# Squares for the query and key norms of band attention: written to an SBUF tile instead of the block's PSUM

## The chip, the core and the metric

The kernel runs on one core of a Trainium2 chip. The metric is the device time of one execution in microseconds; the lower the better. The kernel before takes 2714.26 us (median of 3 runs, 2714.21 to 2715.04).

## What is computed

A trunk of two layers over 256 tokens of width 2048, all in float32. Each layer is a modulated RMS norm, a token mixer with a gated residual, a second modulated norm and a squared-ReLU MLP with a gated residual. The mixer of the first layer runs two groups of heads side by side behind one input projection: eight gated-DeltaNet heads, and eight heads of chunked band attention. The change touches the start of the attention alone, where queries and keys are normed per head:

```python
def chunk_band_attention(q, k, v, q_norm_w, k_norm_w, rel_bias):
    ...
    qh = rms_norm(heads(q), q_norm_w).astype(f32) * (ATT_DH ** -0.5)
    kh = rms_norm(heads(k), k_norm_w).astype(f32)
    ...

def rms_norm(x, w):
    xf = x.astype(jnp.float32)
    y = xf * lax.rsqrt(jnp.mean(xf * xf, axis=-1, keepdims=True) + NORM_EPS)
    return (y * w.astype(jnp.float32)).astype(x.dtype)
```

The mean of squares runs over the 128 channels of one head. Of the squares themselves nothing but these sums is used.

## The kernel before

Weights stream from HBM in pieces of 1 MB through four SBUF buffers (`raw`, SP's queue). Each half of a piece is split into a rounded part `wh` (ScalarE, L317) and a remainder `wl` (VectorE, L321), and TensorE multiplies in three passes (wh by u, wl by u, wh by the remainder of u), all through the helper at L308. Between the weights, VectorE works off the rows of the modulation matrix (`mraw`, L439), each a multiply with a sum over 128x2048.

A projection of 512 columns for 256 tokens is a block. It lands in one PSUM tile `pg` of two banks, one for each 128 tokens; there are two such tiles (pool `psg`), so a third block must wait until the first one's tile is read out. A generator per block (a task) is then stepped along between the matmuls of the following blocks, so that its ScalarE and VectorE work lies beside them. Program order sets priorities; a scheduler then places every instruction on its engine's queue, and the engines run their queues in order.

`att_qk` (L1232) is that task for a block of queries or keys of four heads. It runs four times: for AQ and AK, whose blocks carry a partial sum from earlier (`part`, added by VectorE at L1242), and for AQ+1 and AK+1, whose blocks are copied by ScalarE (L1240). For each half t of 128 tokens it brings the block into an SBUF tile `aq` and takes the squares of four heads (L1244), with the sum of each into a column of the small tile `ass`. The squares go back into the half of the block that has just been read. When both halves are done, VectorE makes the reciprocal root of the eight sums (L1247, then L271 to L276 in three Newton rounds), scales `aq` (L1250), TensorE transposes it (L314, `pm<-ident,aq`) and ScalarE takes the result to SBUF (L1257).

At the same time the DeltaNet heads run in `gdn_tile`: their squares for norms are L1042, the gates `gu` L1046, and their blockwise inversion takes a fresh tile `gY` per level, cleared by GpSimd (L1107). All of these, `aq` among them, come from one pool of 18 SBUF tiles of 2 KB per partition (`s2`): a nineteenth has to wait until one of the 18 has been read for the last time.

Of the kernel before, what the change touches and what calls it, by code (L numbers as in the profile page):

```python
# [13 lines left out]
AF = mybir.ActivationFunctionType  # L14
# [4 lines left out]
P = 128  # L19
# [93 lines left out]
class Trunk:  # L113
# [1118 lines left out]
    def att_qk(self, ps, nw, part=None):  # L1232

        nc = self.nc
        a, v = [], self.small(8, "ass")
        for t in range(2):
            x = self.s2(tag="aq")
            flat = x.rearrange("p h d -> p (h d)")
            if part is None:
                nc.scalar.copy(flat, ps[t])  # L1240
            else:
                nc.vector.tensor_tensor(flat, ps[t], part[:, t], op=ALU.add)  # L1242
            for h in range(4):
                nc.scalar.activation(ps[t][:, h * P : h * P + P], x[:, h], AF.Square, accum_out=v[:, t * 4 + h : t * 4 + h + 1])  # L1244
            a.append(x)
            yield
        nc.vector.tensor_scalar(v, v, 1.0 / P, EPS, op0=ALU.mult, op1=ALU.add)  # L1247
        r = self.rsqrt(v, 8, "a")
        for t in range(2):
            nc.vector.tensor_tensor(a[t], a[t], self.bc(r[:, t * 4 : t * 4 + 4]), op=ALU.mult)  # L1250
        yield
        res = self.unit()
        for t in range(2):
            pt = self.pm()
            for h in range(4):
                self.tr(pt[:, h], a[t][:, h])
            nc.scalar.activation(res[:, :, t * P : t * P + P], pt, AF.Copy, scale=nw)  # L1257
            if t == 0:
                yield
        return res  # L1260
# [551 lines left out]
```

## Time and profile before

| | before |
|---|---|
| median of 3 runs | 2714.26 us |
| the profiled execution | 2719.37 us |
| its span, first to last instruction | 2717.6 us |
| TensorE busy | 2665.0 us (98%) |
| VectorE busy | 2147.6 us (79%) |
| ScalarE busy | 1351.2 us (50%) |
| the 32 squares of `att_qk` | first at 240.0, last at 409.2 us |

Times within the profile count from the start of its span. Busy time is time in which an engine has an instruction under way; the idle time before an instruction is put down to what released it. TensorE's clock is told as a share of full speed (1.00 is 2.4 GHz, 0.50 is 1.2 GHz).

### The profile page before, as it was taken

The page shows a single profiled execution, that of the slowest core. Times are in us where ns is not written, and L with a number is a line of the kernel's source. Part 1 is how long each engine was busy: PE and PEld are TensorE (multiplying, and loading weights), DVE is VectorE, ACT ScalarE, POOL GpSimd, SP SyncE. Part 2 cuts the span into 40 slices and gives each one's busy share as a digit, 9 for nine tenths or more (in the row PEclk, how much of TensorE's full clock was granted, in tenths as well). Part 3 has the DMA queues.
Part 4 walks back from the last instruction along what each step waited for, and adds up shares of the span by engine and source line. Part 5 has one row for each costly group of instructions (what it writes and reads, how often), then busy time and mean ns, then how long its engine had stood idle before and what let it go on. Part 6 is the DMA issues. An engine that isn't in the chain of part 4 may idle for free.

```text
span 2717.6 us, 39677 instructions
## 1 busy us (share of the span) xinstructions
PE 2665.0 (98%) x15664; PEld 2350.4 (86%) x15664; DVE 2147.6 (79%) x3081; ACT 1351.2 (50%) x1976; POOL 24.5 (1%) x98
## 2 busy tenths in 40 slices
PE   5999999999999999999999999999999999999999
PEld 5887989888888888888888888888888888888888
DVE  7998998987888888889889876897777855555554
ACT  3444454546445354454556544665555354454452
POOL 1000000000000000000000000000000000000000
PEclk9999999999999999999999999999999999999999
DMA  9986487867899898988456665554558855555554
GB/s 341 353 325 235 172 301 272 294 241 282 322 339 328 328 336 330 333 331 307 165 185 217 217 234 200 203 185 172 196 177 293 324 201 188 188 191 193 186 192 134
DMA packets 100459, 680.06 MB, mean 250 GB/s; under 512 B 11185, under 2 KB 14513, under 8 KB 19377
## 3 DMA queue, kind: packets, MB, share of 16 engines
q1 hardware_dynamic: 95376, 669.07, 68.5%
q10 hardware_dynamic: 4896, 8.46, 1.0%
q8 instruction: 123, 2.02, 0.3%
q14 instruction: 64, 0.52, 0.1%
HBM read 675.33 MB, written 2.16 MB: 249 GB/s over the span
## 4 chain that ended last, share of the span: by engine, by line
PE 90%; DVE 6%; DMA 1%; ACT 1%; issue 1%; SPq 0%; ACTq 0%; DVEq 0%
PE pw L308 70%; PE pg L308 13%; PE pm L311 4%; PE pm L308 3%; DVE mraw L439 2%; DVE wl L321 1%; PE pm L314 1%; DMA mraw<-in_mod_dram 1%; DVE u L1592 0%; ACT wh L317 0%; DVE hf L862 0%; ACT pm L1042 0%; DMA raw<-in_w_ab_dram 0%; DMA x<-in_x_dram 0%; DVE u L865 0%
## 5 line engine op out<-in xcount | busy, mean ns | idle before, releaser
L317 ACT CAST wh<-raw 128x1024 fp32r<-128x1024 f32 x870 | 907.1, 1051 | 1031.6 <-PE pw L308 732.9
L321 DVE TENSOR_TENSOR wl<-raw,wh 128x1024 fp32r<-128x1024 f32 x870 | 1048.7, 1220 | 463.8 <-ACT wh L317 349.6
L308 PE MATMUL pw<-u,wh 128*128 128x512 f32 x5584 | 1321.6, 391 | 2.6 <-DVE pad L973 1.9
L308 PEld LDWEIGHTS pw<-u,wh 128*128 128x128 f32 x5584 | 1032.2, 188 | 208.2 <-issue 3.3
L308 PEld LDWEIGHTS pw<-u,wl 128*128 128x128 f32 x5584 | 702.3, 191 | 21.3 <-issue 2.1
L308 PE MATMUL pw<-u,wl 128*128 128x256 f32 x5584 | 714.5, 283 | 0.3 <-DVE wl L321 0.3
L439 DVE SCALAR_TENSOR_TENSOR mraw<-mraw,crow 128x2048 f32<-128x2048 f32 x192 | 438.0, 2283 | 17.8 <-DMA mraw<-in_mod_dram 17.5
L308 PE MATMUL pg<-wh,u 128*128 128x512 f32 x864 | 281.6, 397 | 0.0
L308 PEld LDWEIGHTS pg<-wh,u 128*128 128x128 f32 x864 | 161.9, 188 | 32.1 <-issue 0.5
L925 DVE SCALAR_TENSOR_TENSOR x<-pw,mod,x 128x256 f32<-128x256 f32 x352 | 161.1, 478 | 22.6 <-PE pw L308 20.3
L308 PE MATMUL pg<-wl,u 128*128 128x512 f32 x432 | 169.9, 393 | 0.7 <-DVE wl L321 0.5
L308 PE MATMUL pg<-u,wh 128*128 128x256 f32 x672 | 124.6, 285 | 0.0
L308 PEld LDWEIGHTS pg<-u,wh 128*128 128x128 f32 x672 | 105.7, 192 | 0.3
L308 PEld LDWEIGHTS pg<-wl,u 128*128 128x128 f32 x432 | 81.4, 188 | 17.6 <-DVE wl L321 2.1
L308 PE MATMUL pg<-u,wl 128*128 128x256 f32 x336 | 95.3, 284 | 0.0
L308 PE MATMUL pm<-u,wh 128*128 128x256 f32 (+1 forms) x304 | 64.6, 310 | 19.2 <-ACT wh L317 19.2
L308 PEld LDWEIGHTS pm<-u,wh 128*128 128x128 f32 x304 | 49.1, 198 | 20.3 <-ACT wh L317 20.0
L308 PEld LDWEIGHTS pg<-u,wl 128*128 128x128 f32 x336 | 64.4, 192 | 0.1
L984 DVE SCALAR_TENSOR_TENSOR u<-pad,cst,u 128x256 f32<-128x256 f32 x144 | 60.6, 477 | 3.3 <-ACT u L978 3.2
L864 ACT ACTIVATE u<-hf,mod 128x256 fp32r<-128x256 f32 x64 | 29.3, 502 | 53.0 <-DVE hf L862 53.0
L1504 ACT ACTIVATE rl<-rs 128x512 f32<-128x512 f32 x64 | 40.4, 632 | 18.9 <-DVE rs L1499 14.4
L308 PE MATMUL pm<-u,wl 128*128 128x256 f32 x176 | 46.1, 290 | 3.1 <-DVE wl L321 3.1
(299 smaller groups left out, 1580.5 us busy)
## 6 DMA issues: line engine op xcount, KB each, us to landing
raw<-in_w_dram SPq DMA_DIRECT2D x256, 1024.0 KB, 5.0
mraw<-in_mod_dram SPq DMA_DIRECT2D x192, 1024.0 KB, 6.0
raw<-in_w_ab_dram SPq DMA_DIRECT2D x56, 1024.0 KB, 5.7
raw<-in_w_ssd_dram SPq DMA_DIRECT2D x48, 1024.0 KB, 4.9
raw<-in_w_sz_dram SPq DMA_DIRECT2D x32, 1024.0 KB, 4.9
raw<-in_wo_ssd_dram SPq DMA_DIRECT2D x32, 1024.0 KB, 4.8
raw<-in_wo_ab_dram SPq DMA_DIRECT2D x16, 1024.0 KB, 5.2
sE<-sd_rowd ACTq DMA_DIRECT2D x32, 256.0 KB, 4.9
```

The source lines that it names most:

```text
L308: self.nc.tensor.matmul(o, a, b, start=start, stop=stop, skip_group_check=True)
L311: self.nc.tensor.matmul(o, lhsT, rhs, start=True, stop=True, skip_group_check=True)
L314: self.nc.tensor.transpose(o, a, self.ident[:k, :k])
L317: a = self.nc.scalar.copy(hi, src)
L321: b = self.nc.vector.tensor_tensor(lo, src, hi.bitcast(F32), op=ALU.subtract)
L439: x = nc.vector.scalar_tensor_tensor(raw, raw, 1.0, self.crow, op0=ALU.mult, op1=ALU.mult, accum_out=t[:, f : f + 1])
L864: nc.scalar.activation(hi, h[:, f], AF.Identity, bias=shift[:, col])
L925: nc.vector.scalar_tensor_tensor(x[:, 2 * b + f], ps[:, f, n], g[:, 2 * cb + f : 2 * cb + f + 1], x[:, 2 * b + f], op0=ALU.mult, op1=ALU.add)
L984: nc.vector.scalar_tensor_tensor(h, pad[:, f, 1 + q : 257 + q], w[:, q, j : j + 1], h, op0=ALU.mult, op1=ALU.add)
L1504: nc.scalar.activation(rl, lo, AF.Relu)
```

## The change

The squares of `att_qk` no longer go back into the block's PSUM tile. They go to an SBUF tile `asq` of the pool of 18, one for each of the four calls, used by both halves in turn. What is squared, the sums, and the number of instructions are the same; each call asks the pool for three tiles instead of two.

```diff
         nc = self.nc
         a, v = [], self.small(8, "ass")
+        sq = self.s2(tag="asq")
         for t in range(2):
             x = self.s2(tag="aq")
...
             for h in range(4):
-                nc.scalar.activation(ps[t][:, h * P : h * P + P], x[:, h], AF.Square, accum_out=v[:, t * 4 + h : t * 4 + h + 1])
+                nc.scalar.activation(sq[:, h], x[:, h], AF.Square, accum_out=v[:, t * 4 + h : t * 4 + h + 1])
             a.append(x)
             yield
```

## Rows read from the trace of the kernel before

**Rows 1.** The page: busy time of an engine, share of the span, instructions.
```profile
PE 2665.0 (98%) x15664; PEld 2350.4 (86%) x15664; DVE 2147.6 (79%) x3081; ACT 1351.2 (50%) x1976; POOL 24.5 (1%) x98
```
**Rows 2.** Windows of the mixer: stretch, its length; busy by engine; clock, DMA share, GB/s.
```profile
240.00:260.00 20.00, 19.42 (x101) 14.31 (x99) 14.09 (x59) 17.59 (x83) 0.53 (x1) 1.00 0.54 201
...
340.00:380.00 40.00, 39.21 (x201) 32.04 (x200) 38.14 (x92) 25.64 (x87) 2.62 (x5) 1.00 0.81 290
...
420.00:440.00 20.00, 17.98 (x143) 17.64 (x142) 14.16 (x28) 6.19 (x9) 0.31 (x1) 0.91 0.79 270
```
**Rows 3.** TensorE's longest waits from 240 to 520 us: total, times, longest.
```profile
PE pm L314 <- DVE aq L1250: 2.8, 2, 2.0
PE pm L314 <- DVE go L1197: 0.5, 1, 0.5
PE pm L311 <- DVE gd_g L1007: 0.4, 1, 0.4
```
**Rows 4.** ScalarE by line and form: busy us, mean ns; idle before.
```profile
L830 ACT ACTIVATE sq<-x 128x512 f32<-128x512 f32 x24 | 14.7, 628 | 17.1 <-DVE x L925 16.8 <-DMA x<-in_x_dram 0.4
...
L1244 ACT ACTIVATE pg<-aq 128x128 f32<-128x128 f32 x32 | 9.0, 281 | 2.2 <-DVE aq L1242 1.8
...
L818 ACT ACTIVATE sq<-x 128x256 f32<-128x256 f32 x16 | 6.4, 415 | 7.1 <-DVE x L925 6.9
```
**Rows 5.** ScalarE's timeline at 240 and 359 us: start, length, instruction, idle before.
```profile
240.04 0.28 ACT L1244 ACTIVATE pg<-aq 128x128 f32<-128x128 f32 x1 [1.80 <-DVE aq L1242]
...
240.48 0.28 ACT L1244 ACTIVATE pg<-aq 128x128 f32<-128x128 f32 x1
...
359.29 0.28 ACT L1244 ACTIVATE pg<-aq 128x128 f32<-128x128 f32 x1
...
359.58 0.27 ACT L1042 ACTIVATE pm<-pm 128x128 f32<-128x128 f32 x1
...
361.02 0.27 ACT L1244 ACTIVATE pg<-aq 128x128 f32<-128x128 f32 x1
```
**Rows 6.** VectorE's timeline around the block AK.
```profile
253.12 0.69 DVE L1242 TENSOR_TENSOR aq<-pg,u 128x512 f32<-128x512 f32 x1 [3.18 <-ACT pg L1244]
254.53 0.17 DVE L1047 TENSOR_SCALAR gss<-gss 128x8 f32<-128x8 f32 x1 [0.72 <-ACT pm L1042]
```
**Rows 7.** Timelines of VectorE, ScalarE and TensorE around the block AQ+1.
```profile
361.45 0.17 DVE L1247 TENSOR_SCALAR ass<-ass 128x8 f32<-128x8 f32 x1 [1.59 <-ACT pg L1244]
...
363.76 1.29 DVE L1250 TENSOR_TENSOR aq<-aq,ay 128x512 f32<-128x512 f32 x2
...
363.60 1.57 ACT L1046 ACTIVATE gu<-Umask,gd_g 128x128 f32<-128x128 f32 x5
...
364.60 0.63 PE L314 MATMUL pm<-ident,aq 128*128 128x128 f32 x4 [0.79 <-DVE aq L1250]
```
**Rows 8.** Timelines of VectorE and TensorE around AK+1's norm.
```profile
411.82 0.16 DVE L1247 TENSOR_SCALAR ass<-ass 128x8 f32<-128x8 f32 x1
...
423.27 2.29 DVE L439 SCALAR_TENSOR_TENSOR mraw<-mraw,crow 128x2048 f32<-128x2048 f32 x1 [2.24 <-DMA mraw<-in_mod_dram]
...
427.94 1.09 PE L314 MATMUL pm<-ident,aq 128*128 128x128 f32 x4 [2.02 <-DVE aq L1250]
```
**Rows 9.** Window behind that wait.
```profile
427.00:432.00 5.00, 4.06 (x23) 4.09 (x24) 3.72 (x6) 1.65 (x3) 0.00 (x0) 0.66 0.78 298
```
**Rows 10.** Timelines of ScalarE, GpSimd and TensorE: AK+1's copies and squares, cleared tiles.
```profile
395.68 0.58 ACT L1240 COPY aq<-pg 128x512 f32<-128x512 f32 x1 [2.95 <-PE pm L311]
...
409.23 0.28 ACT L1244 ACTIVATE pg<-aq 128x128 f32<-128x128 f32 x1
...
400.69 0.52 POOL L1107 MEMSET gY<- 128x512 f32 x1 [5.35 <-PE pm L311]
...
412.85 0.52 POOL L1107 MEMSET gY<- 128x512 f32 x1 [4.67 <-PE pm L311]
...
415.55 0.28 PE L308 MATMUL pg<-u,wh 128*128 128x256 f32 x1
```

## The prediction

> **What bounds the kernel now.** I read the page first, then windows over the stretch in which the changed line runs, then the waits of TensorE in it, and last the timelines around each of the four calls. The page shows TensorE busy for 2665.0 of 2717.6 us, with VectorE at 79% and ScalarE at 50% [rows 1]. So an edit to ScalarE's work moves the end only where TensorE stands still, or runs at its lower clock, because of it. The windows show how little of that there is while the squares run: TensorE stands still for 0.6 us from 240 to 260, 0.8 us from 340 to 380 and 2.0 us from 420 to 440, where the clock is also below full [rows 2]. The list of waits gives the same by cause: 2.8 us in two waits for the scaled `aq`, which is what `att_qk` makes, 0.5 us for the DeltaNet output, and 0.4 us for its gates [rows 3]. That is the whole stock from which the change can draw: 3.7 us of waits, and what the clock costs behind the longest of them.
>
> **The change part by part.** It adds and removes no instruction but the tile; it moves the output of 32 squares, drops what their output held up, and asks the pool of 18 for one tile more in each call.
>
> *The square itself.* Now, from SBUF to PSUM, it takes 281 ns for 128 columns [rows 4]. From SBUF to SBUF the trace has the same function at 415 ns for 256 and 628 ns for 512 columns, so 0.83 ns a column, and 415 - 107 = 308 ns for 128 [rows 4]. That is 27 ns more, 0.9 us for 32. The Trainium skill says the same of direction (ScalarE: Activation LUTs, section "ACT is a hardware spline evaluator": a ScalarE result reaches PSUM sooner than SBUF) and gives no size; by that rule alone the change could only lose.
>
> *The pace of squares.* Two squares of one half that follow each other directly start 0.44 us apart (240.04, 240.48), while a square and the DeltaNet square behind it, which writes another tile, start 0.29 us apart (359.29, 359.58) [rows 5]. I read the difference as each square waiting for the end of the one before it, since both write into one PSUM tile. Counted in ScalarE's timeline, twelve of the 32 follow a sister directly. If quarters of an SBUF tile are kept apart, as I expect, they gain 12 x 0.15 = 1.8 us, against the 0.9 us above. Both lie on ScalarE, which idles half of the time, and count for nothing by themselves.
>
> *The add that waits.* In AK, VectorE stood for 3.18 us until the last square of the first half, and only then added the second half at 253.12 [rows 6]. The add reads the other bank of the tile that the squares write. With the squares gone from the tile it can run some 3 us earlier. I count it at nothing: TensorE has other matmuls here (its one wait before 260 is the 0.4 us for the gates, upstream of the add), and VectorE's next instruction waits for the DeltaNet squares on ScalarE anyway, 0.72 us at 254.53 [rows 3, 6]. The Trainium skill tells (PSUM — Partial Sum Buffer, section "PSUM bank collisions raise a hardware error") that PSUM needs guarding by bank, and the two halves are two banks. By that rule the add had no need to wait for the squares, and the wait would be for something else and stay. The row, which names the squares, speaks for the tile as a whole; the time is the same by both, but it gives the case below in which nothing changes a little more weight.
>
> *The wait at 364.* For AQ+1, TensorE stands 0.79 us until VectorE has scaled `aq` [rows 7]. The chain behind it is: last square, then VectorE released at 361.45 after 1.59 us of waiting for it, the Newton rounds, the scaling at 363.76. Before it, the four squares of the second half alternated with DeltaNet squares, from 359.29 to 361.02, 0.58 us each [rows 5]. Freed from each other they may stand together, at about 0.31 us each: the last would start at 360.2, 0.8 us sooner. At best this ends the 0.79 us. At worst the order stays, and the gain is nothing. What comes next then is the matmul on `gu`, whose last gate ScalarE finishes at 365.2, with TensorE's 0.63 us of transposes before it [rows 7]; the DeltaNet squares and gates that the four pass would end as much later as these end sooner. I take 0.5 us, between the ends, nearer the upper one since the VectorE row names the square as the last to come.
>
> *The wait at 426.* For AK+1, TensorE stands 2.02 us, again for `aq` [rows 8]. Behind it the granted clock is 0.66 over five microseconds, a mean of its levels of 2.4 and 1.2 GHz, so 5 x 0.34 = 1.7 us of work more is lost [rows 9]. But here the last square starts at 409.23, and VectorE takes up the sums 2.3 us after its end, at 411.82, then gets stuck for 2.24 us behind a modulation row whose transfer has not landed, at 423.27 [rows 8, 10]. Squares that end some tenths earlier change nothing in that. I take 0, with 3.7 us as the upper bound.
>
> *The nineteenth tile.* AK+1's first copy, at 395.68, waited 2.95 us for a matmul that has nothing to do with the block it reads: it waited for a tile of the pool, and so do the clearings of `gY`, at 400.69 to 412.85, for 5.35 and 4.67 us [rows 10]. The pool is full here, and a third tile for the call must come out of one of these places. If the call gives way, its squares slip from one release to the next, at most from 409.5 to about 413. The next block, GZ, which takes the PSUM tile, starts at 415.55 [rows 10], and needs after the change only that the copies are through. VectorE's 411.82 becomes some 413.5 at worst, still ahead of the transfer at 423.27. If `gY` gives way, it is a clearing made many microseconds ahead of its use. I take 0; the price if that cover is gone is 1 us.
>
> *The order of everything behind.* The scheduler places the later instructions anew when 32 instructions have other waits. The trace can't show that. Its bounds are the stalls of this stretch: all of them gone (3.7 + 1.7 = 5.4 us gained), or one such as that at 426 more.
>
> The sum is -0.5 us. The profiled execution would go from 2719.37 to 2718.9; it is 5.1 us above the median of the runs, so on the median's scale 2714.26 - 0.5 = 2713.8.
>
> **The rivals.** *Slower: VectorE's queue falls behind a transfer.* If the new order puts one more modulation row ahead of the Newton rounds or of a weight remainder in the stretch 410 to 430, VectorE waits for its landing as at 423.27 (2.24 us) and works it off (2.29 us), TensorE stands for these 4.5 us, and the low clock costs 1.7 us more [rows 8, 9]: 2714.3 + 6.2 = 2720.5. It decides where TensorE has no more finished weights: it ran out of them once in before. For it speaks that this stall exists; against it that the squares' group comes earlier, if at all.
>
> *Faster: the stalls of the stretch go.* With the add, the squares and the release of the block's tile all sooner, VectorE could be ahead by its 3.18 us when the transfer comes late, and both waits for `aq`, the smaller ones and the clock's loss go: 2714.3 - 5.4 = 2708.9. Against it speaks that from 340 to 380 VectorE is at 95% and has no room to carry a lead over 170 us [rows 2].
>
> *The pool.* The third tile holds the call and the inversion up beyond their cover: 2715.3, as priced above.
>
> *Nothing changes.* The squares still wait for each other in the new tile, the add waits for something else, and the order stays: 2714.3. For it speaks that the PSUM tile seems to be guarded as a whole, and the SBUF tile may be too; against it the row of the add, which names the squares [rows 6].
>
> **How the numbers follow.** The forecast, 2713.8 and two or so microseconds around it, has 0.50; nothing changes 0.10; the pool 0.07; slower 0.21; faster 0.12. The range reaches to both outer cases, 2707 to 2721, and leaves out what lies beyond them. A measurement of this kernel can tell about 0.2%, 5.4 us, from no change. Faster by more takes the faster case in full, 0.12; the slower case lies beyond it, 0.21; the rest is 0.67.
>
> **What would show it.** In the profile after, the squares should take about 308 ns each and follow each other 0.3 us apart; the add of AK should no longer wait for them; TensorE's waits for `aq` should be 2 us rather than 2.8, all of it at AK+1. If squares in a row still start 0.44 us apart, my reading of their waits is wrong. If TensorE's waits between 240 and 520 us differ by more than 2 us from 3.7, the order has moved, and the forecast holds only by luck. If the difference lies after 520 us, I missed where the change reaches.

## The result, and the profile after

The changed kernel takes 2722.04 us (median of 11 runs) against 2715.12 us of the kernel before beside it: ratio 1.0024, 95% interval 1.0015 to 1.0034. It is 6.9 us slower, where 0.5 us less was forecast. The execution shown ahead of the prediction was a long one (2719.37 us, with a stretch at the lower clock); the kernel before was profiled once more as e1 (2714.30 us, none such in the mixer), and "before" below means that profile. The profiled execution of after took 2720.30 us; the spans of the two profiles are 2712.6 and 2718.6 us, 6.0 us apart.

First the edited line itself. The fence shows the squares of after as one group (count; duration in ns, least, median and most; first and last start), then three of them in a row, then AK's add:

```profile
L1245 ACT ACTIVATE asq<-aq x32: 292/294/312, 239.7 to 416.0; 128x128 f32<-128x128 f32 x32
...
240.30 0.29 ACT L1245 ACTIVATE asq<-aq 128x128 f32<-128x128 f32 x1
...
240.59 0.29 ACT L1245 ACTIVATE asq<-aq 128x128 f32<-128x128 f32 x1
...
240.88 0.29 ACT L1245 ACTIVATE asq<-aq 128x128 f32<-128x128 f32 x1
...
253.25 0.17 DVE L1047 TENSOR_SCALAR gss<-gss 128x8 f32<-128x8 f32 x1 [4.07 <-ACT pm L1042]
...
254.76 0.68 DVE L1243 TENSOR_TENSOR aq<-pg,u 128x512 f32<-128x512 f32 x1
```

A square takes 294 ns instead of 281, and squares in a row start 0.29 us apart instead of 0.44 [rows 4, 5]. The add no longer waits for them [rows 6]: it now stands behind VectorE's wait for the DeltaNet squares, 4.07 us long, and so it doesn't start sooner (254.76 against 253.12 us). Each local change is small. The loss is elsewhere. Windows of the four stretches from 360 us on (length; busy time and instructions of TensorE, its weight loads, VectorE, ScalarE and GpSimd; TensorE's clock, DMA share, GB/s), before and then after:

```profile
360.00:380.00 20.00, 19.22 (x102) 15.48 (x101) 18.45 (x59) 11.37 (x37) 2.11 (x4) 1.00 0.75 278
380.00:400.00 20.00, 20.00 (x128) 17.62 (x127) 19.39 (x34) 8.13 (x17) 1.57 (x3) 1.00 0.81 301
400.00:420.00 20.00, 20.00 (x163) 19.06 (x162) 19.69 (x34) 9.49 (x19) 2.10 (x4) 1.00 0.91 332
420.00:440.00 20.00, 19.43 (x168) 19.05 (x168) 17.16 (x32) 8.39 (x18) 0.31 (x1) 1.00 0.79 289
```

```profile
360.00:380.00 20.00, 18.85 (x100) 15.14 (x99) 19.20 (x49) 13.18 (x38) 2.62 (x5) 1.00 0.88 327
380.00:400.00 20.00, 19.46 (x102) 15.91 (x100) 19.86 (x40) 3.18 (x4) 1.05 (x2) 1.00 0.81 311
400.00:420.00 20.00, 16.96 (x141) 15.82 (x140) 19.72 (x29) 11.03 (x28) 2.25 (x5) 1.00 0.92 323
420.00:440.00 20.00, 20.00 (x174) 19.62 (x173) 15.52 (x37) 7.38 (x11) 0.68 (x2) 1.00 0.65 233
```

Between 380 and 420 TensorE of before never stands still and issues 291 matmuls; of after it is busy for 36.42 of 40 us and issues 243. The clock is full in both. The first matmul of the output projection shows that the loss lies ahead of it, in before and in after:

```profile
488.32 1.33 PE L308 MATMUL pw<-u,wh 128*128 128x512 f32 x5
```

```profile
495.19 2.00 PE L308 MATMUL pw<-u,wh 128*128 128x512 f32 x8
```

It starts 6.9 us later. From there to the end of the span after takes 2223.4 us and before 2224.2 us, so nothing is added behind it. TensorE's longest waits between 240 and 520 us (us in total, times, longest), in after:

```profile
PE pm L314 <- DVE gX L1114: 2.2, 2, 1.3
PE pm L314 <- ACT gu L1046: 1.1, 1, 1.1
PE pm L314 <- DVE aq L1251: 0.8, 1, 0.8
PE pg L308 <- ACT aq L1241: 0.7, 1, 0.7
```

Before had none of the first [rows 3]: `gX` is the working tile of the DeltaNet inversion (L1107 to L1119), where each step needs the one before. So the question became why the inversion of the second DeltaNet group (heads 4 to 7) is now in the way. The group has two tiles of 128 tokens, and each makes a `gV` (L1069). Right behind the group's second `gV` VectorE makes the inversion's inputs (L1078 to L1082), so that `gV`, called the second `gV` from here on, tells when the inversion can start. VectorE's timeline, before, with the Newton rounds of AQ+1 and of the group's first tile, and then the second `gV`:

```profile
361.88 0.16 DVE L1047 TENSOR_SCALAR gss<-gss 128x8 f32<-128x8 f32 x1
...
362.31 0.16 DVE L274 TENSOR_TENSOR gt<-gy 128x8 f32<-128x8 f32 x1
362.42 0.17 DVE L276 SCALAR_TENSOR_TENSOR ay<-at,ay 128x8 f32<-128x8 f32 x1
362.51 0.16 DVE L275 TENSOR_TENSOR gt<-gt,gn 128x8 f32<-128x8 f32 x1
362.62 0.17 DVE L274 TENSOR_TENSOR at<-ay 128x8 f32<-128x8 f32 x1
...
381.79 0.68 DVE L1069 TENSOR_TENSOR gV<-pm,gnk 128x512 f32<-128x512 f32 x1
```

After:

```profile
364.55 0.16 DVE L274 TENSOR_TENSOR gt<-gy 128x8 f32<-128x8 f32 x1
364.62 2.29 DVE L439 SCALAR_TENSOR_TENSOR mraw<-mraw,crow 128x2048 f32<-128x2048 f32 x1
...
366.83 0.17 DVE L275 TENSOR_TENSOR gt<-gt,gn 128x8 f32<-128x8 f32 x1
366.91 0.69 DVE L1063 TENSOR_TENSOR gE<-gE,Umask 128x512 f32<-128x512 f32 x1
367.51 0.16 DVE L276 SCALAR_TENSOR_TENSOR gy<-gt,gy 128x8 f32<-128x8 f32 x1
367.59 2.29 DVE L439 SCALAR_TENSOR_TENSOR mraw<-mraw,crow 128x2048 f32<-128x2048 f32 x1
...
389.03 0.68 DVE L1069 TENSOR_TENSOR gV<-pm,gnk 128x512 f32<-128x512 f32 x1
```

The Newton rounds are chains of small steps, 0.2 us each. Before, the attention's chain (`ay`, `at`) and the DeltaNet's (`gy`, `gt`) stand between one another, a step every 0.1 us. After, the attention's chain runs alone, and its scaling begins at 363.12; the DeltaNet's comes behind it, and between its steps stand modulation rows of 2.29 us. The group's first `gV` comes 8.9 us later for it (378.13 against 369.27). Counted from the start of the trace, 53 modulation rows and 82 weight remainders stand ahead of the second `gV` in before, 55 and 84 in after. Two of each are 2 x 2.29 + 2 x 1.22 = 7.0 us, and `gV` is late by 389.03 - 381.79 = 7.2 us.

### The profile page after: what moved, and what is told of

It is laid out like the page before. It is cut to its first block, busy times and chain, and to the rows that moved or that the text cites. A ratio compares the mean times of both kernels' runs of the same rounds, so it can differ in the third digit from the quotient of the medians.

```text
span 2718.6 us, 39708 instructions
## 1 busy us (share of the span) xinstructions
PE 2663.3 (98%) x15664; PEld 2347.2 (86%) x15664; DVE 2150.4 (79%) x3081; ACT 1349.9 (50%) x1976; POOL 24.3 (1%) x98
## 3 DMA queue, kind: packets, MB, share of 16 engines
q8 instruction: 123, 2.02, 0.3%
## 4 chain that ended last, share of the span: by engine, by line
PE 90%; DVE 7%; ACT 1%; issue 1%; DMA 1%; SPq 0%; DVEq 0%; ACTq 0%
PE pw L308 70%; PE pg L308 13%; PE pm L311 3%; PE pm L308 3%; DVE mraw L439 2%; DVE wl L321 2%; PE pm L314 1%; DMA mraw<-in_mod_dram 1%; DVE u L1593 0%; ACT wh L317 0%; DVE hf L862 0%; DMA x<-in_x_dram 0%; DVE u L865 0%; DMA sE<-sd_rowd 0%; ACT pm L1042 0%
```

## The experiments

Every median is of 5 to 11 executions, beside the kernel before on the same chip (medians 2714.66 to 2715.53 us). The table gives the median, its ratio to that before with the 95% interval, and from the profile: when the second `gV` starts, how many rows and remainders stand ahead of it, how long TensorE waits for `gX`, `gXt` and `gY` between 380 and 440 us (a sum of rounded rows), and when the output projection begins.

| kernel | us | ratio | gV | rows, rem. | waits | output |
|---|---|---|---|---|---|---|
| e1 before | 2715.12 | 1.0000 (0.9991-1.0009) | 381.8 | 53, 82 | 0 | 488.3 |
| after | 2722.04 | 1.0024 (1.0015-1.0034) | 389.0 | 55, 84 | 2.2 | 495.2 |
| e2 own tile | 2721.14 | 1.0019 (1.0010-1.0027) | 389.6 | 55, 84 | 2.2 | 494.9 |
| e3 last call alone | 2716.01 | 1.0000 (0.9991-1.0009) | 381.8 | 53, 82 | 0 | 487.6 |
| e4 tile held | 2723.58 | 1.0032 (1.0020-1.0045) | 387.4 | 54, 84 | 3.5 | 496.6 |
| e5 one slot | 2718.43 | 1.0006 (0.9997-1.0015) | 382.5 | 53, 82 | 0 | 490.8 |
| e6 AQ+1 alone | 2723.26 | 1.0025 (1.0015-1.0035) | 389.5 | 55, 84 | 3.4 | 495.8 |
| e7 AQ and AK alone | 2716.38 | 1.0004 (0.9995-1.0013) | 382.9 | 53, 82 | 0 | 488.7 |
| e8 before, Newton late | 2723.50 | 1.0029 (1.0018-1.0041) | 389.5 | 55, 84 | 3.4 | 497.1 |
| e9 DeltaNet squares first | 2723.79 | 1.0031 (1.0021-1.0042) | 391.0 | 55, 84 | 2.2 | 498.8 |
| e10 after, rows held | 2732.31 | 1.0070 (1.0057-1.0083) | 370.6 | 47, 79 | 0 | 492.2 |
| e11 before, rows held | 2734.59 | 1.0072 (1.0059-1.0085) | 373.2 | 48, 80 | 2.4 | 494.2 |
| e12 before, Newton first | 2717.32 | 1.0011 (1.0002-1.0020) | 379.8 | 52, 82 | 0 | 491.1 |
| e13 after, pool of 20 | 2720.64 | 1.0023 (1.0015-1.0032) | 389.0 | 55, 84 | 2.5 | 495.2 |
| e14 before, pool of 20 | 2715.61 | 1.0004 (0.9995-1.0012) | 381.9 | 53, 82 | 0 | 489.6 |
| e15 all but AQ+1 | 2715.19 | 1.0002 (0.9993-1.0011) | 382.3 | 53, 82 | 0 | 488.4 |
| e16 before, smaller dose | 2721.59 | 1.0026 (1.0017-1.0035) | 387.2 | 54, 84 | 3.5 | 496.5 |

The theory at the start was ORDER: VectorE's work ahead of the second DeltaNet group is what costs. Its first rival was POOL, the third tile that each call holds.

**e1, the kernel before again.**

> The kernel before once more, with a second profile of it. Both theories: 2714 to 2716 us, ratio 1.000. What it is for: the profiled execution of before took 2719.4 us, 4 us over its own median, with a stretch at the lower clock at 428 and another near 1378 us. If such stretches come and go from execution to execution, this profile shows fewer or other ones, and the stalls of the mixer alone are compared.

It gave the profile that the comparisons use.

**e2, squares in an SBUF tile outside the pool of 18.**

```diff
-        sq = self.s2(tag="asq")
+        sq = self.s_p.tile([P, 4, P], F32, tag="asq", name=self.nm("asq"), bufs=1)
```

> The change, but the squares go to an SBUF tile of their own beside the pool of 18 (2 KB more), so no call asks the pool for a third tile. Theory POOL (the third tile, asked of a full pool, holds up the copies of AK+1 and with them the next block): back to 2714 to 2717 us, the second copy of AK+1 near 407 us and no wait of TensorE for it. Theory ORDER (squares that no longer wait for each other make the scheduler place modulation rows ahead of the DeltaNet's Newton rounds, the second gV comes at 389 instead of 382 us): stays at 2720 to 2724 us, with gV near 389.

The pool has all its tiles back, and the loss stays.

**e3, the change in AK+1 alone.** AK+1 is where the pool is full.

```diff
-put("k1", self.att_qk(ps, self.knw))
+put("k1", self.att_qk(ps, self.knw, None, True))   # own tile for this call
```

> The change in the last of the four calls (AK+1) alone; the other three write into the block's PSUM as before. POOL: nearly the whole loss stays, 2719 to 2722 us, since only there the pool is full; squares of AK+1 start near 407 and its second copy near 414 us. ORDER: the shift of VectorE's queue lies before that call (from 365 us), so it goes: 2714 to 2717 us, second gV near 382 us.

Nothing is lost. With e2 the third tile is out as the main cause.

**e4, the tile held, three of four squares still in PSUM.**

```diff
-activation(ps[t][:, h * P : h * P + P], x[:, h], AF.Square, ...)
+activation(sq[:, h] if h == 3 else ps[t][:, h * P : h * P + P], x[:, h], AF.Square, ...)
```

> Each call takes the third tile of the pool, but three of its four squares per half still go into the block's PSUM and only the fourth into the tile: the tile is asked for and held as in the change, while squares in a row and the second add wait as before. POOL: 2719 to 2724 us. ORDER: 2714 to 2717 us.

A miss for ORDER as I had put it, which expected the old order from a kernel that leaves most squares in PSUM. But its `gV` is late too, with 54 rows and 84 remainders ahead: one square moved is enough to shift the order, so this kernel doesn't separate the theories.

**e5, the change with the squares made to wait for one another.**

```diff
-activation(sq[:, h], x[:, h], AF.Square, ...)
+activation(sq[:, 0], x[:, h], AF.Square, ...)
```

> The change in all four calls, in the pool's tile, but all four squares of a half write the same quarter of asq, so that each has to wait for the one before, as in the kernel before. IN A ROW (the loss comes because the squares of AQ+1 no longer wait for one another: ScalarE's queue then holds four of them in a row ahead of the DeltaNet squares of line 1042, the DeltaNet tiles' Newton rounds start behind AQ+1's instead of between them, and two more modulation rows and four more weight remainders go in): the squares of line 1245 alternate with those of line 1042 again, second gV of the second DeltaNet group at 381 to 383 us, 2714 to 2717 us. TILE (the place matters: SBUF as destination, a tile of the pool of 18 held, the PSUM no longer guarding the add): 2719 to 2724 us, as after.

The order of before is back. The median, 2718.43 us, lies between the two ranges; it is 2.9 us above before, with an interval of the ratio that includes 1. In the profiled execution TensorE waits 2.00 us for AK+1's scaled `aq`, behind a modulation row whose transfer landed 2.21 us late; that is the stall of [rows 8], which comes and goes with the execution.

**e6 and e7, the change in AQ+1 alone, and in AQ and AK alone.**

```diff
-put("q1", self.att_qk(ps, self.qnw))
+put("q1", self.att_qk(ps, self.qnw, None, True))   # e6
-self.att_qk(ps, self.knw if c0 == AK else self.qnw, part)
+self.att_qk(ps, self.knw if c0 == AK else self.qnw, part, True)   # e7
```

> Squares in an SBUF tile in AQ+1 alone; AQ, AK and AK+1 as before. IN A ROW (AQ+1's squares beside the DeltaNet squares): second gV at 388 to 390 us, 2719 to 2724 us. FIRST TWO (the changed calls AQ and AK, over 100 us sooner, shift what follows): second gV near 382, 2714 to 2717 us.

> Squares in an SBUF tile in AQ and AK alone; AQ+1 and AK+1 as before. IN A ROW: second gV at 381 to 383 us, 2713 to 2717 us. FIRST TWO: second gV at 388 to 390 us, 2719 to 2724 us.

AQ+1 alone carries all of the loss; the two earlier calls carry none that is clear of the noise. e3 and e5 to e7 say which squares matter: those of AQ+1, when they are free of each other.

**e8, the kernel before with the second group's Newton rounds late.** The squares are not touched. A larger number in `priority` puts instructions later in their engine's order.

```diff
+        with self.priority(300 if hg else 0):
             nc.vector.tensor_scalar(v, v, EPS, None, op0=ALU.add)
             rn = self.rsqrt(v, 8, "g")
             ...
```

> The kernel before, squares in PSUM and untouched; only the second DeltaNet group's Newton rounds (lines 1047 to 1055) are given a later priority (+300), so that more modulation rows and weight remainders stand ahead of them on VectorE. ORDER COSTS (late DeltaNet tiles are what costs the time): second gV at 387 to 391 us instead of 381.8 and 2719 to 2725 us. ORDER IS A SIGN ONLY (the time goes elsewhere, to the second copy of AK+1 that waits for a tile of the pool or to the squares themselves): second gV as late, yet 2714 to 2717 us.

This is the direct test: the same 55 and 84 ahead of `gV`, and 8.0 us lost, with every square in PSUM. The order costs the time by itself.

**e9, the change with the DeltaNet squares ahead of AQ+1's.** In after ScalarE's queue holds AQ+1's four squares (359.18 to 360.06) in a row ahead of eight DeltaNet squares (L1042); before, they alternated [rows 5]. I took that for the step that leads to the late Newton rounds, and for what costs the time.

```diff
+            with self.priority(-200 if hg else 0):
                 for h in range(4):
                     nc.scalar.activation(ps[:, h], ps[:, h], AF.Square, ...)
```

> The change in all calls, the four squares of each half still free of one another, but the second DeltaNet group's own squares (line 1042) are given an earlier priority (-200), so that they stand ahead of AQ+1's in ScalarE's queue. VectorE's program then has the Newton rounds of AQ+1 and of the DeltaNet tile between one another again, yet still 55 modulation rows and 84 weight remainders ahead of the second gV, as the change (53 and 82 in the kernel before). QUEUE (what costs the time is that the DeltaNet squares come behind AQ+1's, on ScalarE): second gV back at 381 to 384 us, 2714 to 2717 us. ROWS (what costs the time is the two rows and two remainders more, 2 x 2.29 + 2 x 1.22 = 7.0 us of VectorE, wherever the squares stand): second gV at 387 to 390 us, 2719 to 2724 us.

It is not what costs. The DeltaNet squares are first, 55 rows and 84 remainders still stand ahead of `gV`, and 9.1 us are lost. The run doesn't bring back the alternation of before, though: AQ+1's last four squares now come behind all DeltaNet squares, from 362.53 us.

**e10 and e11, fewer modulation rows in the stretch, after and before.**

```diff
-        self.rate, self.rate2 = 0.25, 1.1
+        self.rate, self.rate2 = 0.25, 0.7
```

> The change in full, with the rate at which modulation rows are taken up from the second group of blocks on cut from 1.1 to 0.7 a step; the rows come later, none is left out. VectorE's program has 47 rows and 79 remainders ahead of the second gV instead of 55 and 84. ROWS: the DeltaNet tiles are no longer late (second gV before 382 us), the output projection begins at 487 to 490 us as in the kernel before, 2713 to 2718 us; up to 3 us more if the later rows are in the way behind 440 us. SQUARES (the loss belongs to the squares in SBUF or the tile of the pool, with the order as a companion): 2719 to 2724 us.

> The control of e10: the kernel before, squares in PSUM, with the same cut of the rate from 1.1 to 0.7; 48 rows and 80 remainders ahead of the second gV instead of 53 and 82. ROWS: with the rows out of the way the change costs nothing, so this and e10 agree within 2 us (ratio of e10 to this 0.9995 to 1.0008). SQUARES: e10 stays 4 us or more above this.

Both are slow, for a reason that I hadn't expected: the rows that are held back are missing at the second norm. TensorE's waits from 560 to 600 us, alike in both:

```profile
PE pm L308 <- ACT sq L818: 13.3, 2, 11.3
```

So the absolute times missed. The output projection, which lies ahead of this wait, begins late too, at 492.2 and 494.2 us instead of 487 to 490, so this wait isn't all of it. The pair was to agree within 2 us and is 2.3 us apart, with the changed kernel the faster: 2732.31 against 2734.59 us. With the rows out of the way the change shows no loss. But e11 waits 2.4 us for the inversion's tiles although its `gV` comes at 373.2, so an early `gV` alone doesn't keep those waits away.

**e12, the kernel before with the Newton rounds first.**

```diff
+        with self.priority(-150 if hg else 0):
             nc.vector.tensor_scalar(v, v, EPS, None, op0=ALU.add)
             ...
```

> The kernel before with the second DeltaNet group's Newton rounds given an earlier priority (-150): one modulation row fewer ahead of both gV (52 and 82 instead of 53 and 82). ROWS with a cushion (TensorE is idle for only 2.7 us between 240 and 520 us, so there is little to win): second gV 2.3 us sooner, near 379.5 us, and 2713 to 2716 us. ROWS without a cushion (each us by which gV moves moves the end): 2712 to 2713.5 us.

`gV` comes 2 us sooner as expected, and nothing is won. The median is 2.7 us above before, with an interval of the ratio just above 1, and above both ranges; no run says why. It gives no sign that the inversion of before came too late.

**e13 and e14, a pool of 20 tiles, after and before.** In every kernel of the first eight that lost time, AK+1's second copy was late as well, at 414.5 us in after against 406.8, waiting for a tile of the full pool. That was a rival to the late inversion, though in e2, e6 and e8 AK+1 asks for no third tile of the pool and has the late copy all the same (414.1 to 414.2 us).

```diff
-        ... tag="s", name=self.nm(tag), bufs=18)
+        ... tag="s", name=self.nm(tag), bufs=20)
```

> The change in full with 20 tiles in the pool instead of 18; VectorE's program still has 55 rows and 84 remainders ahead of the second gV. CHAIN LATE: second gV at 388 to 390 us and 2719 to 2724 us, whether AK+1's second copy waits or not. POOL FULL (AK+1's second copy waits for a tile): that copy at 407 to 409 us instead of 414.5, and 2714 to 2717 us.

> The control: the kernel before with 20 tiles in the pool; 53 rows and 82 remainders ahead of the second gV. Both theories: 2713 to 2717 us; a gain over the kernel before of more than 1.5 us would say that the pool of 18 holds it back too.

With 20 tiles that copy is back at 408, though it still waits for a matmul of the inversion, in e13's timeline:

```profile
408.11 0.59 ACT L1241 COPY aq<-pg 128x512 f32<-128x512 f32 x1 [2.28 <-PE pm L311]
```

The loss stays: `gV` at 389.0, the output projection at 495.2 as in after. TensorE's waits only move within the chain, in e13:

```profile
PE pm L314 <- DVE gX L1114: 1.3, 2, 0.9
PE pm L311 <- DVE gY L1108: 1.2, 1, 1.2
```

**e15, the change everywhere but in AQ+1.**

> Squares in an SBUF tile in AQ, AK and AK+1, in PSUM in AQ+1 alone; 53 rows and 82 remainders ahead of the second gV, as in the kernel before. CHAIN LATE: second gV at 381 to 383 us, 2714 to 2717 us, no gain over the kernel before. If the 3.18 us wait of AK's add and the 2.02 us stall of TensorE at AK+1 were worth anything by themselves: 2711 to 2713 us.

No loss, and no gain: 2715.19 us. AK's add and the stall at AK+1, two of the places where I had looked for a gain, bring nothing that can be measured.

**e16, a smaller dose than e8** (priority later by 100, not 300).

> The kernel before, squares in PSUM, with the second DeltaNet group's Newton rounds at a priority later by 100 (300 in e8): 54 rows and 84 remainders ahead of the second gV, one row and two remainders more than before, 2.29 + 2 x 1.22 = 4.7 us of VectorE. CHAIN LATE, step by step: second gV near 386.5 us and 2718 to 2721 us. CHAIN LATE past a point only (the spare work of TensorE covers so much): second gV near 386.5 us and 2714 to 2717 us.

One row and two remainders more, 4.7 us of VectorE, make `gV` 5.4 us late and cost 6.7 us. The loss isn't clearly smaller than e8's 8.0 us, as I had expected of the smaller dose, and isn't covered either. This is the cleanest of the tests: the squares are in PSUM, the Newton rounds of AQ+1 and of the group's first tile stand between one another as in before, that tile's `gV` is in time (369.64 us), and only the second tile is late.

**What the runs settle.** All eight kernels with 54 or 55 rows and 84 remainders ahead of the second `gV` lost 5.6 to 9.1 us, and TensorE waits 2.2 to 3.5 us for the inversion's tiles in each. All with 52 or 53 and 82 lie within 3 us of before and show no such wait (e10 and e11 stand apart, with another stretch in the way and e11's waits as told). That holds whether the squares are in PSUM (e8, e16) or not. How TensorE loses it can be read from the matmuls of projections (tile `pg`), windows of that tile alone; before:

```profile
390.00:400.00 10.00, 4.06 (x14) 1.98 (x12) 0.00 (x0) 2.21 (x9) 1.00 0.74 273
400.00:408.00 8.00, 2.60 (x8) 1.44 (x8) 0.00 (x0) 1.11 (x4) 1.00 1.00 371
408.00:415.00 7.00, 2.36 (x7) 1.25 (x7) 0.00 (x0) 1.09 (x6) 1.00 0.94 343
```

After:

```profile
390.00:400.00 10.00, 6.58 (x26) 4.32 (x25) 0.00 (x0) 0.00 (x0) 1.00 0.64 233
400.00:408.00 8.00, 0.39 (x2) 0.00 (x0) 0.00 (x0) 0.59 (x1) 1.00 0.86 279
408.00:415.00 7.00, 0.00 (x0) 0.00 (x0) 0.00 (x0) 0.49 (x1) 1.00 0.94 362
```

Before, the block AV+1 is spread over the inversion and fills its pauses up to 415 us. After, the inversion isn't there yet, TensorE uses that block up by 400, and then has the inversion alone until 415, because the next block (GZ) needs the PSUM tile that AK+1 holds until its second copy (L1241). In before a projection matmul stands at 405.38, between two steps of the inversion; in after the next steps come with a pause, and GZ starts right behind AK+1's copy:

```profile
400.00 0.40 PE L308 MATMUL pg<-wh,u 128*128 128x512 f32 x1
...
403.28 0.66 PE L314 MATMUL pm<-ident,gX 128*128 128x128 f32 x4 [0.89 <-DVE gX L1114]
...
409.42 0.66 PE L314 MATMUL pm<-ident,gX 128*128 128x128 f32 x4 [1.32 <-DVE gX L1114]
...
415.15 0.50 PE L308 MATMUL pg<-u,wh 128*128 128x256 f32 x2 [0.68 <-ACT aq L1241]
```

All eight kernels that lost show such a gap between AV+1's last matmul (at 400.0 to 407.6 us) and GZ's first (408.8 to 418.6). In e1, e3, e5, e7, e12, e14 and e15 GZ follows within 0.4 us. But the length of the gap isn't the price: in e13 GZ starts at 408.75, 6.4 us sooner than in after, and the output projection begins at the same 495.2.

**What stays open.** Why two more rows are put ahead of `gV` when AQ+1's squares are free: the order is fixed before the kernel runs, no trace shows the choice, and ScalarE's queue, my guess at the step, doesn't explain it (e9). Rows and remainders rose together in every kernel that lost, so which of them counts isn't separated. Between a `gV` that is 0 to 1.1 us late and one that is 5.4 us late no kernel stands, so where the loss begins isn't known. That a late `gV` costs the time is shown by e8 and e16; how it costs it, the inversion without cover, is read from traces and argued, since no run gave it other cover, and e13 shows that the account isn't complete.

## Why the prediction was wrong, point by point

- *The square itself*: estimated 308 ns, measured 294, 13 ns more than in PSUM and hidden. The Trainium skill's direction (ScalarE: Activation LUTs, section "ACT is a hardware spline evaluator") agrees with these two rows; the size was half of what I took from wider squares.
- *The pace*: right. 0.44 us apart became 0.29 us, and e5, in which they share a quarter, went back to 0.43 us; it was the wait on the sister.
- *The add that waits*: right that the squares hold it no longer and that it counts for nothing, since VectorE then waits for the DeltaNet squares (4.07 us). Wrong that it can run 3 us sooner: it is placed behind that wait and runs at 254.76. The add waited for squares in the other bank [rows 6] and shows no wait for them in after. So the Trainium skill's rule of guarding by bank (PSUM — Partial Sum Buffer, section "PSUM bank collisions raise a hardware error") would not have called for this wait; the row was the one to go by.
- *The wait at 364*: wrong in sign. The scaling of `aq` began 0.7 us sooner (363.12 against 363.83), and so did its transposes (363.95 against 364.67). But TensorE had used up its other matmuls 1.1 us sooner (at 362.81 against 363.88), and stood 1.15 us instead of 0.78. The trace puts the 1.15 down to `gu`, which I had named as next; a part of it ended at 363.89 and the first half of `aq` at 363.81, so the two can't be told apart.
- *The wait at 426*: taken as 0, rightly, but I took the stall for a property of the kernel. It is a matter of the execution: the same program shows 2.02 us in one profile [rows 8] and none in e1's, and e5 shows 2.00. It was over half of my stock of 3.7 us (which left out two waits of 0.2 us).
- *The nineteenth tile*: right as to the cost, by e2 and e13. AK+1's last square came at 416 instead of 409 us, later than the 413 that I gave as the worst, but not because of the third tile: e2, which asks the pool for none, has it at 415.7.
- *The order of everything behind*: **this step failed.** I put it at nothing in the sum, and gave it one stall of 4.5 us and 1.7 us of clock as its bound, taken from the stalls that before has. The loss was 6.9 us without a late transfer and at full clock: two rows and two remainders, 7.0 us of VectorE, ahead of the second `gV`. A changed order isn't bounded by the stalls there are. As I read the traces, it takes cover from a chain that shows no wait in before, since it is covered there.
- *The rival "slower"*: the right kind (modulation rows ahead of Newton rounds), at the wrong place (410 to 430, AK+1, instead of 364 to 389), with half of the count and another price. That 2720.5 is near 2722 is luck. I spoke against it with the squares' group coming earlier; AQ+1's Newton rounds did come earlier, and it was the DeltaNet group's that came later.
- *The other rivals*: "faster" needed stalls of which the longest is no property of the order, "the pool" fell with e2 and e13, and "nothing changes" with the squares 0.29 us apart.
- *What would show it*: this part served. TensorE's waits between 240 and 520 us sum to 6.8 us in after, 3.1 more than the 3.7 that I had named, where 2 us was to be the sign of a moved order (they sum to 2.7 in before). The waits for `aq` were 0.8 us, none of it at AK+1, where I expected 2.

Of the 6.9 us by which the output projection starts later, TensorE's idle time ahead of it makes 4.1 (43.98 us in after, 39.87 in before). The other 2.8 us are busy time. In them 2.0 us are work that only moved: nine matmuls of attention (tiles `as` and `aT`) stand ahead of the output projection in after and behind its start in before. The remaining 0.8 us is busy time of matmuls that both kernels have ahead of it. Behind that start after takes 0.9 us less, which leaves the 6.0 us between the ends of the two profiles.

## What to carry to other kernels

Where the order of instructions is laid out anew at each edit, look first for the chain that shows no wait only because other work covers it, here the DeltaNet inversion beside a VectorE that is 98% busy from 380 to 420 us, and price the edit by what happens if that chain starts later by one or two of the large instructions queued around it. A stall list told little of what this edit could lose. When a change leaves the local costs as forecast and the end moves, count what stands ahead of each chain's first instruction in both traces; then make that order in the old kernel without the edit, as e8 and e16 do.

## What the runs showed of the hardware

ScalarE's square of 128 columns with its sum takes 294 ns into SBUF and 281 ns into PSUM, 187 ns of reading the sum beside it in after. Squares that wait for one another start 0.44 us apart in one PSUM tile (before) and 0.43 us in one quarter of an SBUF tile (e5), free ones 0.29 us, so the wait on a sister costs 0.15 us each time on the same engine. VectorE waited 2.24 us for the landing of one modulation row in one execution [rows 8] and not at all in another of the same program (e1), enough to make or unmake the longest stall of the stretch.
